# Retention output formed transposed with its states from one scan, and the search's exact step and key marking taken block by block behind the third pair's norm

## The chip, the cores and the metric

The kernel runs on one NeuronCore of a Trainium2 chip. The metric is the device time of one execution in microseconds (us). TensorE (PE) multiplies matrices, PEld is its weight load; VectorE (DVE), ScalarE (ACT) and GpSimd (POOL) work elementwise; SyncE (SP) issues DMAs. Each engine takes its instructions in a fixed order, and each waits for semaphores that others raise.

## The reference

One step of a decoder layer on 1024 new prompt tokens and 8 x 4 sample tokens, all in float32. From a normalised, modulated input h, one wide projection gives thirteen parts. Two branches use them and are merged by gates:

```python
# sparse attention: index scores choose 256 keys per query
scores = einsum(relu(qi @ ki.T), wi)          # [1024, 1024], causal
idx    = top_k(scores, 256)                   # keys of each query
y_a    = softmax(q @ k[idx].T / 8) @ v[idx] * silu(za)
# retention, 8 heads of 64, chunks of 128 tokens
scores = (q_c @ k_c.T) * decay_mask
out    = scores @ v_c + (q_c @ state) * q_decay
state  = exp(128 * lg) * state + (k_c * k_decay).T @ v_c
y_r    = group_norm(out) * g_ret * silu(zr)
x      = x + gate * ((sigmoid(ga) * (y_a @ w_pa) + sigmoid(gr) * (y_r @ w_pr)) @ w_out)
```

Outputs are the two token sets, their new keys, values and index keys, and the retention states.

## The kernel before

All of the wide projection runs on TensorE as products of split numbers (each float32 operand is a high and a low part): `project` streams 72 products of 128 x 352 per block of 128 columns (8 row blocks, 3 terms, 3 token chunks) into two banks `pj` in turn, and a `use` function takes each chunk out. `prefetch` loads the next block's weights (`ws`, an SP DMA) and splits them (`wh` on ScalarE, `wl` on VectorE or, one time in three, GpSimd, L195 and L196). After the index scores `SC` (prompt, blocks of 128 queries) and `SCS` (sample) stand in SBUF, three things run side by side: four gate blocks; the retention in four pairs of heads; and the search.

The search (`pick_all`) finds for each query the 256th largest score bit by bit, in 31 rounds. In each, VectorE counts for five blocks how many scores reach a candidate (`count`, L728), ScalarE does the same by signs for the last prompt block and the sample (`count_signs`, L735), and a few small VectorE instructions (L742, L744, L804, L806) make the next candidate. Then come `exact` (L755 to L770), which finds the exact score for the two blocks counted by signs, and `finish` (L775 to L784), which counts the scores above the threshold for all seven blocks and marks by block the keys that are out: equal to the threshold (L780), a running count of these (a scan, L781), two combining steps (L782, L783) and the mask `bi` or `bis` (L784). The sample's mask goes to memory (L823, L825) and is used after the retention, the prompt's masks in the attention later.

The retention takes the pairs p = 0 to 3. For each, `pair` projects keys, queries and values; GpSimd rotates keys and queries (L454 to L456); `to_tokens` turns keys and values by TensorE transposes (L426), which ScalarE copies out (`vtok`, `kd`: L465, L468); the gate part z follows (L477 to L479). Then:

- L485: 16 products, for 8 chunks and 2 heads, k decayed by v, into one bank `pk`, chunk after chunk.
- L487, L489: the states. Seven VectorE steps, each S[c] = S[c-1] * decay + pk[c].
- L496, L501: scores of each chunk, times a decay mask, into two tiles `sT`.
- L508, L511: the output `po`, with tokens on the partitions: 14 products q by state (weights are a 64 x 128 piece of q, 64 columns stream), then 16 products of scores and values (weights are 128 x 128 scores, 64 columns stream).
- L513: one ScalarE copy puts `po` in `O`. The sample tokens' part follows (L517 to L540).
- L545 to L568: the group norm of `O`: mean, square, an inverse root in small VectorE steps, transposes back (L564), and L567, which multiplies by z's gate. L567's third instruction is the last of the pair on VectorE.

Behind each pair come a projection of attention queries (`split_rows`, L392, L393) and two gate blocks. Per pair a constant table `DM` of 128 x 320 numbers is loaded (L433); `RC` holds other constants, the decay of the states among them.

The order of each engine is written out by a planner (`schedule_with_timeline_sim=True`) that follows the program's order and its own timeline; the search is traced last (`back`, `drain`) and so fills what the retention leaves on VectorE and ScalarE. `together` and `tc.issue_after(x)` add edges: what is traced inside is put behind x on x's engine, without a semaphore.

Of the kernel before, what the change touches and what calls it, by code (L numbers as in the profile page):

```python
# [49 lines left out]
R_G, R_GS, R_MB, R_ALL = 0, 4, 8, 16  # L50

M_D, M_S, M_ALL = 0, 256, 320


def shape_constants():
# [32 lines left out]
    for h in range(8):  # L88
# [3 lines left out]
        m[q, :32, M_S + 32 * i:M_S + 32 * i + 32] = np.where(ok, np.exp(lg[h] * f(-4.0)), 0)  # L92
        for a, decay in enumerate((np.exp(lg[h] * (size - f(1.0) - step)) * f(0.125), np.exp(lg[h] * (step + f(1.0))))):
            rot[q, a, rows, :TT] = cos * decay[None, :]
            rot[q, a, rows, TT:] = sin * decay[None, :]
        r[rows, R_G + q] = np.exp(lg[h] * f(128.0))
# [23 lines left out]
def _hybrid_step(ctx, tc, A, outs, dbg):  # L120
# [22 lines left out]
    def pt():  # L143
        return ps.tile([128, 512], F32, name="pt", bufs=2)
# [257 lines left out]


    def retention(gp):
        with ExitStack() as s3:
# [4 lines left out]
            nc.gpsimd.memset(O[:, 8], 0.0)  # L410
            for p in range(4):
                pair(rp, RC, O, p)
# [16 lines left out]
    def pair(rp, RC, O, p):  # L429
# [53 lines left out]
        S = rp.tile([128, 8, 64], F32, name="S")  # L483
        pk = pt().rearrange("p (c e) -> p c e", e=64)
        together([lambda c=c, i=i: nc.tensor.matmul(pk[head[i], c], kd[:, c, head[i]], vtok[:, c, head[i]], start=True, stop=True)  # L485
                  for c in range(8) for i in (0, 1)])
        nc.vector.tensor_copy(S[:, 0], pk[:, 0])  # L487
        for c in range(1, 8):
            nc.vector.scalar_tensor_tensor(S[:, c], S[:, c - 1], RC[:, R_G + p:R_G + p + 1], pk[:, c], op0=OP.mult, op1=OP.add)  # L489
        nc.sync.dma_start(st_out[0, 0, 2 * p:2 * p + 2].rearrange("h d e -> (h d) e"), S[:, 7])  # L490


        sT = []
        for g in (0, 1):
# [12 lines left out]
        po = pl().rearrange("p (i c e) -> p i c e", i=2, c=8)  # L507
        together([lambda c=c, i=i: nc.tensor.matmul(po[:, i, c], qT[head[i], 128 * c:128 * c + 128], S[head[i], c - 1], start=(c == 7), stop=False)  # L508
                  for c in range(7, 0, -1) for i in (0, 1)])
        for g in (0, 1):  # L510
            together([lambda c=c, i=i: nc.tensor.matmul(po[:, i, c], sT[g][:, i, c % 4], vtok[:, c, head[i]], start=False, stop=(c == 7))  # L511
                      for c in range(4 * g, 4 * g + 4) for i in (0, 1)])
        nc.scalar.copy(O[:, :8].rearrange("p c i e -> p i c e"), po)  # L513
# [45 lines left out]
        for g in range(3):  # L559
# [7 lines left out]
            nc.vector.scalar_tensor_tensor(yT[:, sl], p_[:, :n], gT[:, p:p + 1], zsT[:, sl], op0=OP.mult, op1=OP.mult)  # L567
# [736 lines left out]
```

## Time and profile before

| | us |
|---|---|
| median of 3 runs (lowest to highest) | 1173.57 (1172.87 to 1173.94) |
| profiled execution | 1169.95 |
| its span, first to last instruction | 1168.1 |
| busy PE, DVE, ACT, POOL | 1104.2, 669.1, 452.8, 329.6 |
| mean granted TensorE clock | 0.98 |

The slices of the page, 29.2 us each, show where things lie: TensorE is at nine tenths or more in nearly all, and in slice 15 (409 to 438 us) at five tenths; VectorE is at nine tenths from about 175 to 440 us, with the search, and at one to three tenths for a while behind it.

```profile
## 2 busy tenths in 40 slices
PE   4999999999989959999998999999999999989997
...
DVE  6865349999999998113332222211237767477755
ACT  5465445555555311222243333212326666343211
POOL 2413006023311700160332222053114433376000
PEclk9999999999999987999999999999999999999999
```

### The profile page before, as it was taken

To read this page: it belongs to the slowest core of one execution; us is meant where nothing else is said; L and a number is where in the kernel's file an instruction comes from. 1 tells how busy PE (TensorE), PEld (TensorE's weight loads), DVE (VectorE), ACT (ScalarE), POOL (GpSimd) and SP (SyncE) were. 2 spreads that over 40 slices of the span, in tenths; PEclk is the share of its full clock that TensorE was granted. 3 is DMA by queue.
4 is the path that set the end of the run, shared out by engine and by line. 5 is a ranking of instruction groups with operands and counts; after the bars stand their busy time and mean duration, and the time that the engine had idled before them with its cause. 6 is when DMAs were issued, how large, how long until landed. Compare 5 with 4: busy or idle time off the path is not lost. (4 is left out here: it accounts for less than half of the span.)

```text
span 1168.1 us, 20306 instructions
## 1 busy us (share of the span) xinstructions
PE 1104.2 (95%) x8040; PEld 1008.5 (86%) x8040; DVE 669.1 (57%) x1599; ACT 452.8 (39%) x874; POOL 329.6 (28%) x258
## 2 busy tenths in 40 slices
PE   4999999999989959999998999999999999989997
PEld 3899989999879959999998999877888888888786
DVE  6865349999999998113332222211237767477755
ACT  5465445555555311222243333212326666343211
POOL 2413006023311700160332222053114433376000
PEclk9999999999999987999999999999999999999999
DMA  9913234145222422341687567589889841395221
GB/s 306 255 33 109 74 105 139 38 126 140 84 79 93 148 58 80 101 120 29 220 269 237 178 205 213 154 294 305 266 245 237 233 135 55 123 299 176 106 97 54
DMA packets 157892, 181.51 MB, mean 155 GB/s; under 512 B 18837, under 2 KB 129501, under 8 KB 156710
## 3 DMA queue, kind: packets, MB, share of 16 engines
q1 hardware_dynamic: 147864, 144.51, 41.7%
q0 software_dynamic: 9856, 35.66, 9.2%
q8 instruction: 63, 1.03, 0.4%
q14 instruction: 31, 0.25, 0.1%
q10 hardware_dynamic: 78, 0.06, 0.0%
HBM read 137.81 MB, written 38.60 MB: 151 GB/s over the span
## 5 line engine op out<-in xcount | busy, mean ns | idle before, releaser
L209 PE MATMUL pj<-hh,wh 128*128 128x352 f32 x1176 | 387.7, 330 | 7.6 <-ACT kx L395 3.0
L211 PE MATMUL pj<-hh,wl 128*128 128x352 f32 x1176 | 383.1, 326 | 0.0
L210 PE MATMUL pj<-hl,wh 128*128 128x352 f32 x1176 | 382.6, 325 | 0.0
L209 PEld LDWEIGHTS pj<-hh,wh 128*128 128x128 f32 x1176 | 223.0, 190 | 17.1 <-issue 6.0
L210 PEld LDWEIGHTS pj<-hl,wh 128*128 128x128 f32 x1176 | 223.7, 190 | 3.3 <-issue 2.5
L211 PEld LDWEIGHTS pj<-hh,wl 128*128 128x128 f32 x1176 | 223.0, 190 | 3.9 <-issue 3.4
L728 DVE TENSOR_SCALAR_CACHE_REDUCE eq<-sc,cand 128x896 bf16<-128x896 f32 (+4 forms) x155 | 135.7, 875 | 2.3
L196 POOL TENSOR_TENSOR wl<-ws,wh 128x1024 fp32r<-128x1024 f32 (+1 forms) x33 | 63.6, 1930 | 190.9 <-ACT wh L195 172.6
L195 ACT CAST wh<-ws 128x1024 fp32r<-128x1024 f32 (+1 forms) x65 | 61.1, 940 | 108.4 <-PE pj L210 66.9
L196 DVE TENSOR_TENSOR wl<-ws,wh 128x1024 fp32r<-128x1024 f32 x32 | 39.9, 1247 | 86.8 <-ACT wh L195 86.8
L1065 POOL TENSOR_SCALAR lg<-lg,st 128x1024 f32<-128x1024 f32 (+7 forms) x64 | 47.5, 749 | 75.3 <-DVE st L1064 69.6
L735 ACT ACTIVATE ra<-sc,cand 128x1024 bf16<-128x1024 f32 x31 | 35.6, 1149 | 64.9 <-DVE cand L806 64.9
L911 POOL DMA_INDIRECT kv<-in_cache_k,idx x32 | 30.9, 966 | 102.0 <-PE str L941 84.0
L1063 ACT ACTIVATE lg<-lg,st 128x1024 f32<-128x1024 f32 (+7 forms) x64 | 49.5, 775 | 21.4 <-DVE st L1062 21.2
L943 DVE COPY kt<-str 128x512 f32<-128x512 f32 x32 | 22.1, 689 | 61.3 <-PE str L941 57.6
L911 POOL DMA_INDIRECT kv<-in_cache_v,idx x32 | 31.4, 981 | 71.0 <-PE sx L969 41.8
L1241 PE MATMUL pj<-wol,MH 128*128 128x512 f32 (+1 forms) x136 | 51.2, 377 | 0.0
L1240 PE MATMUL pj<-woh,MH 128*128 128x512 f32 (+1 forms) x136 | 51.2, 377 | 0.0
L1242 PE MATMUL pj<-woh,ML 128*128 128x512 f32 (+1 forms) x136 | 51.2, 377 | 0.0
L574 ACT ACTIVATE raw<-pj 128x352 f32<-128x352 f32 x48 | 22.1, 460 | 71.9 <-PE pj L211 68.7
L1078 PE MATMUL tr<-C,lg 128*128 128x128 f32 x288 | 43.8, 276 | 1.3 <-ACT pT L1080 0.5
L1078 PEld LDWEIGHTS tr<-C,lg 128*128 128x128 f32 x288 | 33.7, 140 | 8.7 <-ACT pT L1080 1.9
(337 smaller groups left out, 2055.6 us busy)
## 6 DMA issues: line engine op xcount, KB each, us to landing
ws<-in_w_in SPq DMA_DIRECT2D x51, 512.0 KB
TG<-raw SPq DMA_DIRECT2D x16, 528.0 KB
rot<-in_rot SPq DMA_DIRECT2D x8, 1056.0 KB
wa<-in_w_ada SPq DMA_DIRECT2D x16, 512.0 KB
u<-TG SPq DMA_DIRECT2D x8, 528.0 KB
RT<-u SPq DMA_DIRECT2D x8, 528.0 KB
t<-TG SPq DMA_DIRECT2D x8, 528.0 KB
u<-RT SPq DMA_DIRECT2D x8, 528.0 KB
```

Of the source, the lines that this page charges most:

```text
L195: nc.scalar.copy(wh[:, :, :n], ws[:, :, :n])
L196: (nc.vector if len(order) % 3 else nc.gpsimd).tensor_sub(wl[:, :, :n], ws[:, :, :n], f32(wh[:, :, :n]))
L209: nc.tensor.matmul(p, wh[:, k], HH[k][:, sl], start=(k == 0), stop=False)
L210: nc.tensor.matmul(p, wh[:, k], HL[k][:, sl], start=False, stop=False)
L211: nc.tensor.matmul(p, wl[:, k], HH[k][:, sl], start=False, stop=(k == KT - 1))
L728: nc.vector.tensor_scalar(junk[:n, :W], sc, thr[:n, j:j + 1], 0.0, op0=op, op1=OP.add, accum_out=cnt[:n, j:j + 1])
L911: nc.gpsimd.indirect_dma_start(out=t.rearrange("p s c -> p (s c)"), out_offset=None, in_=cache.rearrange("g (r s) h d -> (g r) (s h d)", s ...
L1063: nc.scalar.activation(l, l, AF.Exp, bias=st[:, 2:3], scale=0.125, accum_out=st[:, 3:4])
L1078: nc.tensor.transpose(x[:, 128 * (j - j0):128 * (j - j0) + 128], lg[:, j % 2, 128 * (j // 2):128 * (j // 2) + 128], ident)
L1240: nc.tensor.matmul(x, MH[:, k, tk], wh[:, k], start=(k == 0), stop=False)
L1241: nc.tensor.matmul(x, MH[:, k, tk], wl[:, k], start=False, stop=False)
L1242: nc.tensor.matmul(x, ML[:, k, tk], wh[:, k], start=False, stop=(k == KT - 1))
```

## The change

*States from one scan.* L485's products write `pk` with the chunk as the innermost index (every eighth word of the bank). One VectorE scan over 512 columns, S[j] = m[j] * S[j-1] + pk[j], makes all states; the factors m, zero where a chunk row begins, are a new part of `DM` (now 832 columns), and the column of decays leaves `RC`. Two ScalarE copies per pair put the states into a tile `SD` that is cleared once for the retention and holds for each chunk a 128 x 128 block with the two heads on its diagonal. The last state goes out from `SD`, one DMA per head.

*Output transposed.* `po` now has the heads' channels on the partitions and tokens along the bank: 7 products of a whole `SD` block with q, then 16 of values (128 x 64 weights) with scores (128 columns stream). By halves, ScalarE copies `po` to SBUF, four transposes turn it, and ScalarE copies it into `O`.

*The search's end.* `exact` takes one block (its small steps on one column), `finish` too (its count and remainder for this block, then the same five steps). `pick_all` traces exact(1), exact(0) and finish(6) to finish(0) behind the third pair's last norm step (`normed[2]`, L567) on VectorE.

```diff
@@ -47,9 +47,9 @@
 C_HM = C_SB8 + 16
 C_ALL = C_HM + 32
-R_G, R_GS, R_MB, R_ALL = 0, 4, 8, 16
-M_D, M_S, M_ALL = 0, 256, 320
+R_GS, R_MB, R_ALL = 0, 4, 12
+M_D, M_S, M_G, M_ALL = 0, 256, 320, 832
 def shape_constants():
@@ -90,10 +90,11 @@
         rows = slice(64 * i, 64 * i + 64)
         m[q, :, M_D + 128 * i:M_D + 128 * i + 128] = np.where(df >= 0, np.exp(lg[h] * f(-128.0)), 0)
         m[q, :32, M_S + 32 * i:M_S + 32 * i + 32] = np.where(ok, np.exp(lg[h] * f(-4.0)), 0)
+        m[q, rows, M_G:M_G + 512] = np.where(np.arange(512)[None, :] % 8 > 0, np.exp(lg[h] * f(128.0)), 0)
         for a, decay in enumerate((np.exp(lg[h] * (size - f(1.0) - step)) * f(0.125), np.exp(lg[h] * (step + f(1.0))))):
             rot[q, a, rows, :TT] = cos * decay[None, :]
             rot[q, a, rows, TT:] = sin * decay[None, :]
-        r[rows, R_G + q] = np.exp(lg[h] * f(128.0))
         r[rows, R_GS + q] = np.exp(lg[h] * f(4.0))
     r[:32, R_MB:R_MB + 8] = (t[:, None] // 4 == b[None, :]).astype(f)
     return c, r, m, rot
@@ -400,6 +401,8 @@
             nc.sync.dma_start(d[128 * p:128 * p + 128], f32(t[:, :T]))
     TG = dram.tile([2 * D, TT], F32, name="TG")
+    normed = {}
     def retention(gp):
         with ExitStack() as s3:
@@ -408,8 +411,10 @@
             nc.sync.dma_start(RC, A["rcs"])
             O = rp.tile([128, 9, 2, 64], F32, name="O")
             nc.gpsimd.memset(O[:, 8], 0.0)
+            SD = rp.tile([128, 8, 128], F32, name="SD")
+            nc.gpsimd.memset(SD, 0.0)
             for p in range(4):
-                pair(rp, RC, O, p)
+                pair(rp, RC, O, SD, p)
                 split_rows(gp, O_QA + 128 * p, p, QD, qs)
                 gates(gp, (4 + 2 * p, 5 + 2 * p))
@@ -426,7 +431,7 @@
                 nc.tensor.transpose(p[:n, t - 4 * g], src[:, t * 128:t * 128 + n], ident)
             use(4 * g, m, 128 if g < 2 else NS, p)
-    def pair(rp, RC, O, p):
+    def pair(rp, RC, O, SD, p):
         flat = lambda t: t.rearrange("p t c -> p (t c)")[:, :TT]
         head = [slice(64 * i, 64 * i + 64) for i in (0, 1)]
         DM = rp.tile([128, M_ALL], F32, name="dm")
@@ -480,14 +485,15 @@
         project(O_ZR + 128 * p, use_z)
-        S = rp.tile([128, 8, 64], F32, name="S")
-        pk = pt().rearrange("p (c e) -> p c e", e=64)
-        together([lambda c=c, i=i: nc.tensor.matmul(pk[head[i], c], kd[:, c, head[i]], vtok[:, c, head[i]], start=True, stop=True)
+        S = rp.tile([128, 512], F32, name="S")
+        pk = pt()
+        by_chunk = pk.rearrange("p (e c) -> p c e", c=8)
+        together([lambda c=c, i=i: nc.tensor.matmul(by_chunk[head[i], c], kd[:, c, head[i]], vtok[:, c, head[i]], start=True, stop=True)
                   for c in range(8) for i in (0, 1)])
-        nc.vector.tensor_copy(S[:, 0], pk[:, 0])
-        for c in range(1, 8):
-            nc.vector.scalar_tensor_tensor(S[:, c], S[:, c - 1], RC[:, R_G + p:R_G + p + 1], pk[:, c], op0=OP.mult, op1=OP.add)
-        nc.sync.dma_start(st_out[0, 0, 2 * p:2 * p + 2].rearrange("h d e -> (h d) e"), S[:, 7])
+        nc.vector.tensor_tensor_scan(S, DM[:, M_G:M_G + 512], pk, 0.0, op0=OP.mult, op1=OP.add)
+        for i in (0, 1):
+            nc.scalar.copy(SD[head[i], :, head[i]], S[head[i]].rearrange("p (e c) -> p c e", c=8))
+            nc.sync.dma_start(st_out[0, 0, 2 * p + i], SD[head[i], 7, head[i]])
         sT = []
@@ -504,13 +510,22 @@
             sT.append(t)
-        po = pl().rearrange("p (i c e) -> p i c e", i=2, c=8)
-        together([lambda c=c, i=i: nc.tensor.matmul(po[:, i, c], qT[head[i], 128 * c:128 * c + 128], S[head[i], c - 1], start=(c == 7), stop=False)
-                  for c in range(7, 0, -1) for i in (0, 1)])
+        po = pl()
+        together([lambda c=c: nc.tensor.matmul(po[:, 128 * c:128 * c + 128], SD[:, c - 1], qT[:, 128 * c:128 * c + 128],
+                                               start=(c % 4 == 3), stop=False) for c in range(7, 0, -1)])
         for g in (0, 1):
-            together([lambda c=c, i=i: nc.tensor.matmul(po[:, i, c], sT[g][:, i, c % 4], vtok[:, c, head[i]], start=False, stop=(c == 7))
+            together([lambda c=c, i=i: nc.tensor.matmul(po[head[i], 128 * c:128 * c + 128], vtok[:, c, head[i]], sT[g][:, i, c % 4],
+                                                        start=False, stop=(c % 4 == 3))
                       for c in range(4 * g, 4 * g + 4) for i in (0, 1)])
-        nc.scalar.copy(O[:, :8].rearrange("p c i e -> p i c e"), po)
+        oT = flat(big(rp, "tmp"))[:, :1024]
+        for g in (0, 1):
+            half = slice(512 * g, 512 * g + 512)
+            nc.scalar.copy(oT[:, half], po[:, half])
+            x = pt()
+            for j in range(4):
+                c0 = 512 * g + 128 * j
+                nc.tensor.transpose(x[:, 128 * j:128 * j + 128], oT[:, c0:c0 + 128], ident)
+            nc.scalar.copy(O[:, 4 * g:4 * g + 4].rearrange("p t i e -> p (t i e)"), x)
         qm = rp.tile([128, NB, NS], F32, name="qm")
@@ -564,7 +579,7 @@
                 nc.tensor.transpose(p_[:, (t % 4) * 128:(t % 4) * 128 + n], y2[:n, t], ident[:n, :n])
             n = 512 if g < 2 else NS
             sl = slice(512 * g, 512 * g + n)
-            nc.vector.scalar_tensor_tensor(yT[:, sl], p_[:, :n], gT[:, p:p + 1], zsT[:, sl], op0=OP.mult, op1=OP.mult)
+            normed[p] = nc.vector.scalar_tensor_tensor(yT[:, sl], p_[:, :n], gT[:, p:p + 1], zsT[:, sl], op0=OP.mult, op1=OP.mult)
         nc.sync.dma_start(YR[128 * p:128 * p + 128], yT)
@@ -747,41 +762,41 @@
                 for j, (sc, bi, n, W) in enumerate(AB):
                     nc.vector.tensor_scalar(dst[:n, NV + j:NV + j + 1], cnt[:n, NV + j:NV + j + 1], W - 510.5, no, op0=OP.is_gt, op1=OP.mult)
-        def exact():
+        def exact(j):
+            sc, bi, n, W = AB[j]
+            c = slice(NV + j, NV + j + 1)
+            t, lw, fl = base.bitcast(F32)[:, c], low[:, c], flag[:, c]
+            nc.vector.tensor_scalar(lw, t, 0.0, None, op0=OP.is_lt)
+            nc.vector.scalar_tensor_tensor(lw, t, 1.1754943508222875e-38, lw, op0=OP.is_ge, op1=OP.add)
+            nc.vector.tensor_tensor(t, t, lw, op=OP.mult)
+            count(base.bitcast(F32), OP.is_gt, [(NV + j, AB[j])])
+            up = tp.tile([128, LK], F32, name="eq", bufs=1)
+            ra = tp.tile([128, LK], F32, name="ra", bufs=1)
+            nc.vector.tensor_scalar(up[:n, :W], sc, t[:n], 3.4e38, op0=OP.is_le, op1=OP.mult)
+            nc.vector.tensor_tensor_reduce(out=ra[:n, :W], in0=up[:n, :W], in1=sc, scale=1.0, scalar=3.4e38,
+                                           op0=OP.add, op1=OP.min, accum_out=lw[:n])
+            nc.vector.tensor_scalar(fl, cnt[:, c], 255.5, None, op0=OP.is_ge)
+            nc.vector.tensor_tensor(lw, lw, fl, op=OP.mult)
+            nc.vector.tensor_scalar(fl, fl, -1.0, 3.4e38, op0=OP.add, op1=OP.mult)
+            nc.vector.tensor_tensor(lw, lw, fl, op=OP.add)
+            nc.vector.tensor_tensor(t, t, lw, op=OP.max)
+        def finish(j):
+            sc, bi, n, W = (VB + AB)[j]
             thr = base.bitcast(F32)
...
+            count(thr, OP.is_gt, [(j, (sc, bi, n, W))])
+            nc.vector.tensor_scalar(rem[:, j:j + 1], cnt[:, j:j + 1], -1.0, float(TOPK), op0=OP.mult, op1=OP.add)
+            eq = tp.tile([128, LK], F32, name="eq", bufs=1)
+            ra = tp.tile([128, LK], F32, name="ra", bufs=1)
+            t = thr[:n, j:j + 1]
+            nc.vector.tensor_scalar(eq[:n, :W], sc, t, None, op0=OP.is_equal)
+            nc.vector.tensor_tensor_scan(ra[:n, :W], eq[:n, :W], eq[:n, :W], 0.0, op0=OP.add, op1=OP.bypass)
+            nc.vector.scalar_tensor_tensor(ra[:n, :W], ra[:n, :W], rem[:n, j:j + 1], eq[:n, :W], op0=OP.is_gt, op1=OP.mult)
+            nc.vector.scalar_tensor_tensor(ra[:n, :W], sc, t, ra[:n, :W], op0=OP.is_lt, op1=OP.add)
+            nc.vector.tensor_scalar(bi, ra[:n, :W], MASKNEG, None, op0=OP.mult)
         nc.vector.memset(BI[1], 0.0)
         for b in (0, 1):
@@ -804,8 +819,12 @@
                 nc.vector.tensor_tensor(base, base, inc, op=OP.bitwise_xor)
                 if k > 0:
                     nc.vector.tensor_scalar(cand, base, 1 << (k - 1), None, op0=OP.bitwise_xor)
-            exact()
-            finish()
+            with tc.issue_after(normed[2].ins):
+                exact(1)
+                exact(0)
+                for j in range(NP - 1, -1, -1):
+                    finish(j)
         back.append(pick_all)
         gates(gp, range(4))
```

## Rows read from the trace of the kernel before

**Rows 1.** Busy time of each engine over the whole span (the page, part 1).
```profile
PE 1104.2 (95%) x8040; PEld 1008.5 (86%) x8040; DVE 669.1 (57%) x1599; ACT 452.8 (39%) x874; POOL 329.6 (28%) x258
```

**Rows 2.** Who TensorE waited for, 90 to 700 us: total, times, longest.
```profile
PE pl L508 <- DVE S L489: 12.6, 1, 12.6
PE pt L426 <- ACT tmp L441: 4.1, 2, 2.4
...
PE pj L209 <- ACT raw L574: 1.0, 1, 1.0
```

**Rows 3.** Table by stage: stretch, length, busy time of each engine, clock, DMA.
```profile
388.50:455.50 67.00, 54.38 (x398) 52.10 (x396) 66.19 (x89) 11.39 (x22) 16.95 (x8) 0.82 0.26 77
478.50:529.60 51.10, 51.10 (x327) 50.64 (x325) 4.80 (x4) 12.68 (x24) 22.40 (x11) 1.00 0.37 105
```

**Rows 4.** VectorE in order of time, third pair and search's end: start, us, instruction.
```profile
388.55 2.33 DVE L755 TENSOR_SCALAR low<-base 128x2 f32<-128x2 f32 x1
...
415.54 4.39 DVE L781 TENSOR_TENSOR_SCAN ra<-eq 32x1056 f32<-32x1056 f32 x1
...
430.32 0.22 DVE L487 COPY S<-pt 128x64 f32<-128x64 f32 x1
...
436.49 1.21 DVE L781 TENSOR_TENSOR_SCAN ra<-eq 128x512 f32<-128x512 f32 x1
...
438.46 0.27 DVE L489 SCALAR_TENSOR_TENSOR S<-S,rc,pt 128x64 f32<-128x64 f32 x1
...
454.88 0.61 DVE L784 TENSOR_SCALAR bi<-ra 128x896 bf16<-128x896 f32 x1
```

**Rows 5.** TensorE in order of time, third pair's products and those after them.
```profile
414.50 1.15 PE L485 MATMUL pt<-vtok,kd 128*64 128x64 f32 x32
...
438.88 3.25 PE L508 MATMUL pl<-S,qrT 64*128 64x64 f32 x28 [12.62 <-DVE S L489]
442.06 7.09 PE L511 MATMUL pl<-vtok,tmp 128*128 128x64 f32 x32
...
450.07 0.49 PE L209 MATMUL pj<-hh,wh 128*128 128x352 f32 x1
450.37 0.49 PE L210 MATMUL pj<-hl,wh 128*128 128x352 f32 x1
```

**Rows 6.** TensorE in order of time, fourth pair.
```profile
524.53 1.03 PE L426 MATMUL pt<-C,krT 128*128 128x128 f32 x8
...
529.58 1.15 PE L485 MATMUL pt<-vtok,kd 128*64 128x64 f32 x32
...
538.04 1.78 PE L508 MATMUL pl<-S,qrT 64*128 64x64 f32 x28
539.75 3.79 PE L511 MATMUL pl<-vtok,tmp 128*128 128x64 f32 x32
```

**Rows 7.** Chain that ended last, in order of time: one of the attention's products.
```profile
900.14 2.12 PE po L1095 x36
```

**Rows 8.** ScalarE in order of time, first pair.
```profile
207.23 0.59 ACT L468 COPY kd<-pt 128x512 f32<-128x512 f32 x1
...
218.94 1.15 ACT L735 ACTIVATE ra<-sc,cand 128x1024 bf16<-128x1024 f32 x1 [4.92 <-DVE cand L806]
```

**Rows 9.** Groups by line on VectorE, 388 to 456 us: busy, mean ns, idle before.
```profile
L196 DVE TENSOR_TENSOR wl<-ws,wh 128x1024 fp32r<-128x1024 f32 x2 | 2.4, 1214 | 0.0
...
L527 DVE TENSOR_TENSOR ss<-pl,dm 32x64 f32<-32x64 f32 x1 | 0.2, 205 | 0.0
```

**Rows 10.** GpSimd in order of time, beside the old and the new place.
```profile
415.04 2.68 POOL L196 TENSOR_TENSOR wl<-ws,wh 128x1024 fp32r<-128x1024 f32 x1 [6.42 <-ACT wh L195]
...
498.74 2.45 POOL L454 TENSOR_TENSOR krT<-krT,rot 128x1056 f32<-128x1056 f32 x1 [14.15 <-DMA tmp<-krT]
```

**Rows 11.** VectorE in order of time, last norm step of third and fourth pair.
```profile
478.12 0.25 DVE L567 SCALAR_TENSOR_TENSOR tmp<-pt,gT,zsT 128x32 f32<-128x32 f32 x1 [2.74 <-PE pt L564]
...
570.40 0.25 DVE L567 SCALAR_TENSOR_TENSOR tmp<-pt,gT,zsT 128x32 f32<-128x32 f32 x1 [2.71 <-PE pt L564]
```

More of the change, by code (lines that the diff above doesn't have):

```diff
@@ L748, in reached @@
                     nc.vector.tensor_scalar(dst[:n, NV + j:NV + j + 1], cnt[:n, NV + j:NV + j + 1], W - 510.5, no, op0=OP.is_gt, op1=OP.mult)
-        def exact():
-            thr = base.bitcast(F32)
-            nc.vector.tensor_scalar(low[:, aa], thr[:, aa], 0.0, None, op0=OP.is_lt)
-            nc.vector.scalar_tensor_tensor(low[:, aa], thr[:, aa], 1.1754943508222875e-38, low[:, aa], op0=OP.is_ge, op1=OP.add)
-            nc.vector.tensor_tensor(thr[:, aa], thr[:, aa], low[:, aa], op=OP.mult)
-            count(thr, OP.is_gt, [(NV + j, x) for j, x in enumerate(AB)])
-            for j, (sc, bi, n, W) in enumerate(AB):
-                up = tp.tile([128, LK], F32, name="eq", bufs=1)
-                ra = tp.tile([128, LK], F32, name="ra", bufs=1)
-                c = slice(NV + j, NV + j + 1)
-                nc.vector.tensor_scalar(up[:n, :W], sc, thr[:n, c], 3.4e38, op0=OP.is_le, op1=OP.mult)
-                nc.vector.tensor_tensor_reduce(out=ra[:n, :W], in0=up[:n, :W], in1=sc, scale=1.0, scalar=3.4e38,
-                                               op0=OP.add, op1=OP.min, accum_out=low[:n, c])
-            nc.vector.tensor_scalar(flag[:, aa], cnt[:, aa], 255.5, None, op0=OP.is_ge)
-            nc.vector.tensor_tensor(low[:, aa], low[:, aa], flag[:, aa], op=OP.mult)
-            nc.vector.tensor_scalar(flag[:, aa], flag[:, aa], -1.0, 3.4e38, op0=OP.add, op1=OP.mult)
-            nc.vector.tensor_tensor(low[:, aa], low[:, aa], flag[:, aa], op=OP.add)
-            nc.vector.tensor_tensor(thr[:, aa], thr[:, aa], low[:, aa], op=OP.max)
@@ L772, in finish @@
-        def finish():
-            thr = base.bitcast(F32)
-            count(thr, OP.is_gt, enumerate(VB + AB))
-            nc.vector.tensor_scalar(rem, cnt, -1.0, float(TOPK), op0=OP.mult, op1=OP.add)
-            for j, (sc, bi, n, W) in reversed(list(enumerate(VB + AB))):
-                eq = tp.tile([128, LK], F32, name="eq", bufs=1)
-                ra = tp.tile([128, LK], F32, name="ra", bufs=1)
-                t = thr[:n, j:j + 1]
-                nc.vector.tensor_scalar(eq[:n, :W], sc, t, None, op0=OP.is_equal)
-                nc.vector.tensor_tensor_scan(ra[:n, :W], eq[:n, :W], eq[:n, :W], 0.0, op0=OP.add, op1=OP.bypass)
-                nc.vector.scalar_tensor_tensor(ra[:n, :W], ra[:n, :W], rem[:n, j:j + 1], eq[:n, :W], op0=OP.is_gt, op1=OP.mult)
-                nc.vector.scalar_tensor_tensor(ra[:n, :W], sc, t, ra[:n, :W], op0=OP.is_lt, op1=OP.add)
-                nc.vector.tensor_scalar(bi, ra[:n, :W], MASKNEG, None, op0=OP.mult)
+        def exact(j):
[16 more added lines that the diff above has]
+            nc.vector.tensor_tensor(t, t, lw, op=OP.max)
```

## The prediction

> **What bounds the kernel.** Read the busy shares first: TensorE is busy for 95% of the span and no other engine passes 57% [rows 1]. So an edit counts by TensorE work that it takes away, or by a gap in it that it closes. Then read who TensorE waited for in the stretch that the change touches: one wait is far above the rest, 12.6 us of the third pair's product with the state (L508) for VectorE's state steps (L489); the others before it are five groups from 4.1 down to 1.0 us, 10.6 in all [rows 2]. The table by stage says why. From 388.5 to 455.5 VectorE is busy for 66.19 of 67 us and the clock is 0.82; in the stretch from the third pair's last norm step to the fourth pair's state product it is busy for 4.80 of 51.10 [rows 3]. VectorE's instructions show the cause: L755, the first of the exact step, starts at 388.55; the third pair's first state step (L487) at 430.32, although its product (L485) had ended at 415.65; the sixth step, which L508 needs, at 438.46 [rows 4, 5]. Search work sits between any two of them. L508 starts at 438.88 after 12.62 us of nothing.
>
> That gap costs more than itself, because TensorE comes back slow: L508 takes 3.25 us, in the undisturbed fourth pair 1.78; L511 7.09 against 3.79; the projection products after them follow each other at 0.30 (450.07, 450.37), 12 in all, where the fourth pair's stage has 327 instructions in 51.10 us, 0.16 each [rows 3, 5, 6]. Over these: 1.47 + 3.30, and 12 x 0.14, 1.6. [...]
>
> **The change, part by part.** The sum is made against the profiled execution, 1169.95 us (span 1168.1 and 1.85 around it). The median of the runs shown is 1173.57, 3.6 higher; I carry the difference over to it.
>
> *Third pair's gap.* The exact step and the marking of keys go behind the third pair's norm on VectorE, so nothing of the search stands before that pair's state any more, and VectorE, which ends its counting at about 388, has 25 us of spare time ahead of it. The 12.6 and the 6.4 us go: **-19.0**. Next to be late there is the new chain, short since VectorE and ScalarE are both free.
>
> *TensorE's own work, for each pair.* L511's 16 products (32 instructions) load 64 columns and stream 128 where they loaded 128 and streamed 64. The attention's L1095 has this form: 36 instructions in 2.12 us, 0.059 each [rows 7], so 1.9 instead of 3.79. L508's 28 instructions become 14 with full 128x128 weights; at L511's rate for such weights (3.79/32 = 0.118) that is 1.7 against 1.78. Added are eight transposes; eight in one go take 1.03 [rows 6], in two goes with two run-outs I take 1.3. Sum -0.7, four pairs **-2.8**. The state product L485 now writes every eighth word of its bank. No row shows a strided write by TensorE; below, nothing excludes a gain but nothing suggests one, so 0; above, as much again as it takes now, 1.15 [rows 6], or 4.6 for four pairs. I take 0 because L485's 32 instructions are issued at 0.036 each, and keep 4.6.
>
> [...]
>
> *State chain.* VectorE loses one copy (0.22) and seven steps of some 0.27 (2.1) and gains one scan over 512 columns, 1.21 by the scan of that width in the marking [rows 4]. ScalarE gains two copies into the block-diagonal tile and, for the output, four half-copies instead of one over 1024 columns; at 0.59 for 128x512 that is some 2.5 more per pair [rows 8]. In the first two pairs both engines are also in the search, and ScalarE stands up to 4.92 us on the next candidate (L735) with later copies queued behind it; the products with the state, the transposes and the projections behind them on TensorE wait for those copies. Against that the chain of six steps, spread over 8 us by search work, becomes one. Bounds for both pairs together: -3 (part of the 10.6 us of small waits goes) and +4 (one extra stand of nearly that length). I take **+1.0**.
>
> *The moved block.* Its length: from 388.55 to the end of L784 at 455.49 is 66.9 us [rows 4]. Of that, seven groups of other work, L196's 2.4 the largest and L527's 0.2 the smallest, make 9.6 [rows 9]. Six of its instructions are 11.5 us longer than their like; the first is L755 (2.33 for two columns, where 0.16 is usual), the last the scan at 415.54 (4.39, 2.27 for the same width less 32) [rows 4], and each overlaps a GpSimd instruction, as that scan overlaps L196 at 415.04 [rows 10]. Left are 45.8; per-block small steps, 14 more at 0.22, make it 48.8. It moves past no queue but VectorE's and issues no DMA; SyncE's copy of the first mask (L823, L825) is later with it but read only after the retention, and the weight loads queued behind it are one projection (72 products at 0.16) ahead: 0.
>
> Where it now starts: the fourth pair's norm ends 41.1 us after its state product starts (570.65 - 529.58) [rows 6, 11]; the third's will too, less 4 us for the shorter chain (8.5 us from L485 to L508 become 4.5). The fourth pair's state product comes 115.1 us after the third's (414.50 to 529.58), less 19.0 and 0.7: 95.4. So the block has 95.4 - 37.1 = 58.3 us, 1.1 more until the state product has ended, and about 3 more while TensorE does the scores. It needs 48.8 and the 4.8 of other work; but GpSimd's 22.40 us of rotation and weight work now lie beside it [rows 3, 10]. Beside the old place GpSimd was busy for 16.95 us and cost VectorE 11.5, a share of 0.68; so 15.2 more. 68.8 against 62.4: the fourth pair's scan comes 6.4 us late, and TensorE waits there. With the slow clock after it in the old proportion (6.4 x 6.4/12.6 = 3.3): **+9.7**. Bounds: 0, when GpSimd's work meets the counts, which it does not lengthen, or lies outside; and, with all 22.4 lost, 13.6 of gap and 6.4 of clock, 20.0.
>
> *The rest.* The larger per-pair table (832 columns for 320) is loaded while the pair before is still being finished, the clearing of the tile comes once on an idle GpSimd, the state goes out in eight DMAs for four: 0, and about 1 us if that cover fails. Behind the retention TensorE stays the bound, so I let the gain through.
>
> Sum: -19.0 - 2.8 + 1.0 + 9.7 = **-11.1**, 1158.9 for the profiled execution, **1162.5** by the median.
>
> **The rivals.**
> *A: the block fits.* GpSimd's instructions fall beside the counts, or the norm ends earlier than 37 us. For it: VectorE has only 4.8 us of other work there [rows 3]. Against it: 22.40 us of GpSimd. No new gap: 1162.5 - 9.7 = 1152.8.
> *B: the wait moves and grows; slower.* Place: the fourth pair's L508. The norm ends as late as the third pair's did in the profile, 39.5 us after L508 against 32.6 [rows 5, 6, 11], so 6.9 later, and all of GpSimd's work is lost: a gap of 13.6 + 6.9 = 20.5 and 6.4 of clock, 26.9; -19.0 - 2.8 + 1.0 + 26.9 = +6.1, 1179.7. It decides from a gap of about 14.4 us on. Against it: VectorE has nothing beside that norm any more.
> *C: the strided state product costs.* 4.6 more than the forecast, 1167.1. [...]
> *D: the first two pairs wait for ScalarE.* Each pair has three new hand-overs (tile, output, transposed output), each stands 2 us on the search's candidates: 12 instead of 1, 1173.5. For it: L735's stand of 4.92 [rows 8]. Against it: TensorE has projections to put between.
> That the block would not move at all is excluded by the order edge to the norm.
>
> **How the numbers follow.** A measurement here can tell about 0.2%, 2.3 us, from no change. Chances: forecast 0.42, A 0.27, B 0.09, C 0.10, D 0.12. Faster: nearly all of the forecast and of A, C less 0.02, 0.05 of D: 0.80. Same: the edges of all but A: 0.11. Slower: most of B and a rest of D: 0.09. The range runs from a little under A, where the first pairs also gain, 1151, to the upper end of D, 1174; B lies outside. The forecast's own range is 1157 to 1168.
>
> **What would show it.** Right: no wait at the third pair's L508, and clock 1.0 in its stage; L511 near 1.9 us; VectorE full from the third norm on, and a gap of 3 to 10 us before the fourth pair's L508 with VectorE's scan or ScalarE's copies as what ended it. Wrong: no gap there (A) or one over 14 us (B); L485 much over 1.15 us (C); new waits for ScalarE in the first two pairs that sum to over 5 us (D).

## The result and the profile after

The changed kernel takes 1155.31 us (median of 4 runs, 1153.97 to 1158.47), the kernel before 1173.22 beside it (4 runs, 1172.63 to 1173.94): a ratio of 0.9851, 95% interval [0.9828, 0.9874], 17.9 us less. Forecast were 1162.5 us with a range from 1151 to 1174. The profiled execution took 1154.27 us, against 1169.95 before and 1158.9 forecast for it. All lines below L430 have moved by a few; the state product L485 is L491, the product with the state L508 is L514, the scores' product L511 is L517.

The busy shares hardly move [rows 1]: TensorE is still the bound, busy for 14 us less. First the page's part 1, then who TensorE waited for from 90 to 700 us (total, times, longest).

```profile
PE 1090.3 (95%) x8016; PEld 993.7 (86%) x8016; DVE 674.0 (58%) x1585; ACT 465.1 (40%) x894; POOL 335.0 (29%) x259
```

```profile
PE pl L514 <- ACT SD L495: 12.6, 2, 11.4
PE pj L210 <- ACT qrT L446: 3.2, 2, 1.9
PE pt L431 <- ACT tmp L446: 2.5, 1, 2.5
PE pj L210 <- ACT qs L398: 1.6, 2, 0.9
PE pj L210 <- ACT kx L396: 1.2, 1, 1.2
PE pt L551 <- ACT O L528: 0.7, 1, 0.7
```

The 12.6 us stand there again as in [rows 2], by chance the same figure, but they are another wait: 11.4 of them belong to the fourth pair, and it is ScalarE's copies of the state that end it. TensorE in order of time shows both pairs: the third runs through, the fourth has the gap.

```profile
408.82 1.15 PE L491 MATMUL pt<-vtok,kd 128*64 128x64 f32 x32
...
414.53 1.72 PE L514 MATMUL pl<-qrT,SD 128*128 128x128 f32 x14
416.19 1.97 PE L517 MATMUL pl<-tmp,vtok 128*64 128x128 f32 x32
...
422.04 1.09 PE L527 MATMUL pt<-C,tmp 128*128 128x128 f32 x8
...
503.68 1.15 PE L491 MATMUL pt<-vtok,kd 128*64 128x64 f32 x32
...
520.91 3.35 PE L514 MATMUL pl<-qrT,SD 128*128 128x128 f32 x14 [11.35 <-ACT SD L495]
524.20 2.82 PE L517 MATMUL pl<-tmp,vtok 128*64 128x128 f32 x32
```

The table by stage (stretch, length, busy time of each engine, clock, DMA) shows why, beside [rows 3]: from the third pair's last norm step to the fourth pair's state product VectorE went from 4.80 us of work to 55.64 of 56.2, and in the next 23 us TensorE is busy for half.

```profile
447.50:503.70 56.20, 56.20 (x360) 55.74 (x358) 55.64 (x74) 13.61 (x26) 24.98 (x10) 1.00 0.37 107
503.70:527.00 23.30, 11.95 (x127) 11.07 (x128) 17.38 (x23) 3.65 (x6) 3.46 (x2) 0.71 0.16 44
```

VectorE in order of time gives the moved block: from 447.45 to 515.58, 68.1 us (68.8 forecast). The fourth pair's scan (L493) comes at 517.35, though its product had ended at 504.83. In the middle four lines show what makes the block long: three steps of the marking over 384 columns take 2.65, 2.72 and 1.95 us (0.62, 0.62 and 0.36 in the version without the rotation, below), a count over 512 takes its usual time (0.73; 0.74 in that version).

```profile
447.45 0.21 DVE L772 TENSOR_SCALAR low<-base 128x1 f32<-128x1 f32 x2
...
475.53 2.65 DVE L797 SCALAR_TENSOR_TENSOR ra<-ra,rem,eq 128x384 f32<-128x384 f32 x1
478.22 2.72 DVE L798 SCALAR_TENSOR_TENSOR ra<-sc,base,ra 128x384 f32<-128x384 f32 x1
480.86 0.73 DVE L743 TENSOR_SCALAR_CACHE_REDUCE eq<-sc,base 128x512 bf16<-128x512 f32 x1
...
481.53 1.95 DVE L799 TENSOR_SCALAR bi<-ra 128x384 bf16<-128x384 f32 x1
...
514.95 0.63 DVE L799 TENSOR_SCALAR bi<-ra 128x896 bf16<-128x896 f32 x1
...
517.35 1.22 DVE L493 TENSOR_TENSOR_SCAN S<-dm,pt 128x512 f32<-128x512 f32 x1
```

GpSimd in order of time has the rotation of the fourth pair's keys just there, and ScalarE the two copies that let TensorE go on.

```profile
474.60 3.16 POOL L459 TENSOR_TENSOR krT<-krT,rot 128x1056 f32<-128x1056 f32 x1 [15.77 <-DMA tmp<-krT]
477.73 2.80 POOL L460 TENSOR_TENSOR tmp<-tmp,rot 128x1056 f32<-128x1056 f32 x1
480.60 2.65 POOL L461 TENSOR_TENSOR krT<-krT,tmp 128x1056 f32<-128x1056 f32 x1
```

```profile
518.60 2.26 ACT L495 COPY SD<-S 64x512 f32<-64x512 f32 x2 [3.85 <-DVE S L493]
```

Both L797 and L798 end within half a microsecond of a GpSimd instruction's end (0.42 us behind L459's and 0.41 behind L460's). These two steps with two inputs took 2.65 and 2.72 us for 0.62, while the count (one tensor) beside L461 took 0.73 as elsewhere. But one tensor is no protection by itself: L799, the mask, has one and took 1.95 us for 0.36, until 0.23 us behind L461's end. What makes the one longer and not the other no run shows.

Where the time went is seen best by taking the same projection product in both traces and noting how much later it starts than in the kernel before (us, so earlier is negative; each time counts from its own trace's first instruction). The two parts of the change done alone, and the version with the old seven steps, are experiments below:

```
up to (before's time)               after    retention alone  search alone  seven steps
first pair's state, 200 us          -1.0         +0.4            -1.0          -0.1
first pair, 275 us                  -2.4         -1.0            +0.9          -2.0
second pair, 381 us                 -9.4         -8.2            +1.2          -3.8
third pair, 485 us                 -25.8         -6.3           -18.2         -23.6
fourth pair, 581 us                -12.7         -7.1            +0.5         -10.4
key copies, 726 us                 -15.9        -10.4            +0.6         -13.5
whole span                         -15.6         -9.9            +0.5          -9.7
```

What a stage gives is the difference of two rows: the first two pairs give the changed kernel 8.4 us (-9.4 less -1.0). Up to 200 us the kernels do the same, so the differences of up to 1.0 us there are the single execution's. The search's end alone leaves every engine's order up to 388 us as it was before, and still it loses 2.2 us in the first two pairs: differences of that size between two executions stand for nothing. The 8.4 us do stand: in the ten profiled versions here that have the whole of the new retention they lie between 8.0 and 8.7, and against the search's end alone they would be 2.2 more.

### The profile page after: what moved, and what is told of

Its sections match the earlier page's. It is cut to its first block, busy times and chain, and to the rows that moved or that the text cites. A ratio compares the mean times of both kernels' runs of the same rounds, so it can differ in the third digit from the quotient of the medians.

```text
span 1152.5 us, 20285 instructions
## 1 busy us (share of the span) xinstructions
PE 1090.3 (95%) x8016; PEld 993.7 (86%) x8016; DVE 674.0 (58%) x1585; ACT 465.1 (40%) x894; POOL 335.0 (29%) x259
## 5 line engine op out<-in xcount | busy, mean ns | idle before, releaser
L197 POOL TENSOR_TENSOR wl<-ws,wh 128x1024 fp32r<-128x1024 f32 (+1 forms) x33 | 63.1, 1913 | 174.8 <-ACT wh L196 156.4
L197 DVE TENSOR_TENSOR wl<-ws,wh 128x1024 fp32r<-128x1024 f32 x32 | 41.4, 1294 | 62.2 <-ACT wh L196 61.3
L962 ACT COPY kt<-str 128x512 f32<-128x512 f32 x32 | 18.8, 589 | 55.1 <-PE str L960 44.1
```

The source lines that it names most:

```text
L197: (nc.vector if len(order) % 3 else nc.gpsimd).tensor_sub(wl[:, :, :n], ws[:, :, :n], f32(wh[:, :, :n]))
```

## The experiments

The theory: both gaps are one thing, VectorE late for a pair's state because search work stands before it. The fourth pair's gap is the length of the moved block, stretched by GpSimd. Rival 1: the new chain of scan and ScalarE copies makes that gap. Rival 2: the change is worth what its order is worth, and the retention's new form adds little.

**The retention alone.** The old form of the exact step and of the marking stands in its old place.

```diff
-            with tc.issue_after(normed[2].ins):
-                exact(1)
-                exact(0)
-                for j in range(NP - 1, -1, -1):
-                    finish(j)
+            exact()
+            finish()
```

> One part alone: the new retention (strided state product, one scan, block-diagonal copies, transposed output), with the exact step and the marking left where the kernel before has them, in front of the third pair. Theory (VectorE's order sets both gaps): the third pair's product with the state (L514) waits again, for the scan that stands behind the search end: 14 to 18 us of gap and some 6 of slow clock after it, since only one step instead of six is late but the chain reaches TensorE earlier; no gap over 2 us at the fourth pair. Gain against before only from TensorE's work (3 us) and from the first two pairs and the third's shorter chain (6 to 10): 1161 us, 1157 to 1166. Rival 1 (the new chain of scan and ScalarE copies makes the gap of the fourth pair): that gap stays above 8 us here too. Rival 2 (the gain is the order's alone): 1171 to 1175.

1157.48 us, ratio 0.9875 [0.9852, 0.9899]. The gap is back at the third pair, 9.96 us, and the fourth pair has none (L514 at 528.91, 1.72 us). First TensorE, then VectorE, in order of time.

```profile
426.18 3.36 PE L514 MATMUL pl<-qrT,SD 128*128 128x128 f32 x14 [9.96 <-ACT SD L495]
```

```profile
421.96 0.73 DVE L795 TENSOR_SCALAR eq<-sc,base 128x1024 f32<-128x1024 f32 x1
422.62 1.20 DVE L493 TENSOR_TENSOR_SCAN S<-dm,pt 128x512 f32<-128x512 f32 x1
```

The place is as the theory has it, the size is not: 9.96 for 14 to 18. Rival 1 falls, and so does rival 2: most of the gain is here, without the move. What the move adds in the new retention, 0.9875 to 0.9851, can't be told from nothing: the intervals overlap.

**The search's end alone.** The old retention (state by seven steps, output not transposed); exact step and marking as changed.

```diff
-        nc.vector.tensor_tensor_scan(S, DM[:, M_G:M_G + 512], pk, 0.0, op0=OP.mult, op1=OP.add)
+        nc.vector.tensor_copy(S[:, 0], pk[:, 0])
+        for c in range(1, 8):
+            nc.vector.scalar_tensor_tensor(S[:, c], S[:, c - 1], RC[:, R_G + p:R_G + p + 1], pk[:, c], op0=OP.mult, op1=OP.add)
...
```

> The other part alone: the old retention (seven steps, output not transposed) with the exact step and the marking by block behind the third pair's norm. Theory: the third pair's gap of 12.6 us and its slow clock go (-19), and the fourth pair's product waits as in the changed kernel or a little longer, 12 to 16 us, since its seven steps follow the block; with its slow clock some 16 to 20. Nothing gained in the first two pairs: 1170 us, 1165 to 1175. Added to the retention alone, the two differences make about the whole (-18) or less. Rival 1 (the new chain makes the fourth pair's gap): no gap over 3 us here, time 1152 to 1157.

1170.17 us, ratio 0.9987 [0.9970, 1.0004]: no difference that can be told. The table says why: the third pair gave 19.4 us (19.0 forecast), the fourth took 18.7 back. Two waits stand there, TensorE in order of time:

```profile
523.07 0.66 PE L209 MATMUL pj<-hh,wh 128*128 128x352 f32 x1 [3.61 <-ACT zsT L480]
...
531.50 3.25 PE L510 MATMUL pl<-S,qrT 64*128 64x64 f32 x28 [7.47 <-DVE S L491]
534.68 7.09 PE L513 MATMUL pl<-vtok,tmp 128*128 128x64 f32 x32
```

So the move by itself only moved the gap. The theory holds; rival 1 expected no gap here.

**The changed kernel without the fourth pair's rotation** (for its queries and its keys; that pair's output is another).

```diff
-            nc.gpsimd.tensor_tensor(x, x, RT_[:, :TT], op=OP.mult)
-            nc.gpsimd.tensor_tensor(y, y, RT_[:, TT:], op=OP.mult)
-            nc.gpsimd.tensor_tensor(x, x, y, op=OP.add)
+            if p < 3: nc.gpsimd.tensor_tensor(x, x, RT_[:, :TT], op=OP.mult)
+            if p < 3: nc.gpsimd.tensor_tensor(y, y, RT_[:, TT:], op=OP.mult)
+            if p < 3: nc.gpsimd.tensor_tensor(x, x, y, op=OP.add)
```

> The changed kernel without the fourth pair's rotation of its queries and keys (three GpSimd instructions for each of the two are left out, so that pair's output is another). Theory (the moved block is long because VectorE loses time beside GpSimd): the block takes 55 to 60 us instead of 68.1, its steps in the stretches at 474 to 483 and 489 to 499 take their usual times, the fourth pair's gap of 11.35 us falls to 0 to 3, time 1143 to 1147. Rival 1 (the gap is the new chain's): gap stays over 8 us, time 1153 to 1156. Rival 2 (the block is too long by its own work): block over 63 us, gap about 7, time 1149 to 1152.

1141.46 us, ratio 0.9749 [0.9729, 0.9770]. VectorE in order of time: the block runs from 446.69 to 503.69, 57.0 us instead of 68.1, and L797 over 384 columns takes 0.62. TensorE has no gap.

```profile
446.69 0.21 DVE L772 TENSOR_SCALAR low<-base 128x1 f32<-128x1 f32 x2
...
474.77 0.62 DVE L797 SCALAR_TENSOR_TENSOR ra<-ra,rem,eq 128x384 f32<-128x384 f32 x1
...
503.07 0.62 DVE L799 TENSOR_SCALAR bi<-ra 128x896 bf16<-128x896 f32 x1
```

Six instructions of GpSimd, 18.3 us together, had cost VectorE 11.1 us net, a share of 0.61 (0.68 in the forecast). This is the theory shown: the same chain, no gap.

**The exact step not bound to the norm.** TensorE's, ScalarE's and GpSimd's order is that of the changed kernel.

```diff
+            exact(1)
+            exact(0)
             with tc.issue_after(normed[2].ins):
-                exact(1)
-                exact(0)
```

> The changed kernel, but the exact step of the two blocks that need it is not bound to the third pair's norm; only the marking is. TensorE's, ScalarE's and GpSimd's order is that of the changed kernel. Theory (VectorE is late for the fourth pair by the length of the bound block): the block is shorter by the exact step's 9 us, so the fourth pair's gap falls from 11.35 us to 1 to 4 and its slow clock with it; VectorE has idle time for the exact step ahead of the third pair, which is not late by it: 1143 to 1148. Rival 1 (the gap is the new chain's): no change of the gap, 1154 to 1157. Rival 2 (the exact step in front of the third pair delays that pair instead): a new gap of 4 to 9 us at the third pair's L514, 1150 to 1156.

1145.14 us, ratio 0.9779 [0.9759, 0.9799], as the theory had it; both rivals fall (third pair's L514 at 414.32 without a wait). The fourth pair's gap is gone altogether, but a new wait stands in its stage, for the lower half of a weight block that VectorE forms between two marking steps, all three beside GpSimd's rotation of the queries. TensorE, then VectorE, in order of time:

```profile
494.11 0.43 PE L212 MATMUL pj<-hh,wl 128*128 128x352 f32 x1 [3.64 <-DVE wl L197]
```

```profile
487.67 3.03 DVE L797 SCALAR_TENSOR_TENSOR ra<-ra,rem,eq 128x768 f32<-128x768 f32 x1
490.62 3.43 DVE L197 TENSOR_TENSOR wl<-ws,wh 128x1024 fp32r<-128x1024 f32 x1
```

**The block behind the fourth pair's norm**, whole, and in a second version its marking alone, with the exact step not bound. The diff is that of the first.

```diff
-            with tc.issue_after(normed[2].ins):
+            with tc.issue_after(normed[3].ins):
```

> The changed kernel with the whole block (exact step and marking) behind the fourth pair's norm instead of the third's. Theory (both gaps are VectorE late for a pair's state): no gap at either pair's L514; the fourth pair's 11.35 us and its 2.5 us of slow clock go, 13.9; behind that norm VectorE has 35 us of work in 140, so the block of some 57 to 60 us is hidden there. 1139 to 1144 if nothing else waits. Rival: SyncE stands on its copy of the first mask (L842) until that block is marked, about 10 us after the norm, with the weight loads of the gates queued behind it, and TensorE waits for the weights: 3 to 8 us of new waits, 1144 to 1150.

> Exact step not bound (as in the version with that alone, 1145.14) and the whole marking behind the fourth pair's norm. Theory: no gap at the third and fourth pair's L514, and the 3.6 us wait for the lower half of the weights (VectorE's L197 beside GpSimd's rotation) of that version goes too: 1138 to 1142. Rival: SyncE's stand on the first mask delays the gates' weights by 3 to 8 us: 1143 to 1149, no better than the exact step alone.

1178.38 us, ratio 1.0048 [1.0030, 1.0067], and 1177.19, 1.0029 [1.0012, 1.0046]: both slower than before, by 0.3 to 0.5%. A miss, by theory and rival alike. The gaps at the states are gone (no wait of TensorE from 400 to 560 us); it loses behind. The waits from 90 to 700 us, then VectorE and ScalarE in order of time, in the whole block's version:

```profile
PE pj L210 <- ACT kx L396: 13.6, 3, 9.4
```

```profile
574.03 0.52 DVE L394 TENSOR_TENSOR raw<-pj,raw 128x352 fp32r<-128x352 f32 x1
...
599.71 0.38 DVE L920 TENSOR_SCALAR idx<-gidx 128x8 int32<-128x8 int32 x4
```

```profile
574.58 0.45 ACT L396 COPY kx<-pj 128x352 f32<-128x352 f32 x1 [7.82 <-DVE raw L394]
```

In the changed kernel VectorE is busy for only 16.71 of the 60 us from 560 to 620, but each piece is awaited at once: ScalarE's copy of the new keys stands 7.82 us for VectorE's L394, queued behind marking. And the gathers' indices (L920) are made at 599.71 instead of 515.49, so that the gathers start at 600.14 instead of 555.10. From 800 to 900 us TensorE is then busy for 89.3 us, in the changed kernel for 96.8. In the whole block's version the projection products start 27.6 us earlier than before at 550 us, 16.1 at 650 and 14.9 at 780, and the whole span is 7.6 longer: more is lost behind 780 us than at the key copies. That this later loss comes from the late gathers was not tried by itself.

**Only the last two blocks behind the fourth norm.**

```diff
-                for j in range(NP - 1, -1, -1):
+                for j in range(NP - 1, 1, -1):
                     finish(j)
+            with tc.issue_after(normed[3].ins):
+                finish(1)
+                finish(0)
```

> The changed kernel with the marking of the last two blocks (1 and 0 in its order, 13 us) behind the fourth pair's norm, the rest behind the third's as it is. Theory: the block behind the third pair's norm ends at about 502 instead of 515.6, before the fourth pair's state product has ended (504.83), so the gap of 11.35 us and its slow clock go: 1139 to 1144, as with the rotation left out (1141.46). Rival (the fourth pair waits for something else besides): a gap over 4 us stays, 1146 to 1152.

1150.02 us, ratio 0.9799 [0.9781, 0.9816]. The fourth pair's gap is gone, as expected, but the time falls short of the 1139 to 1144 us: at 581 us the same projection product is 13.3 us earlier than in the changed kernel, at 726 still 7.4, over the whole span 2.7. Among the waits behind the fourth pair are 5.0 us for L396 (1.2 in the changed kernel) and 2.3 for the gathered keys, the loss of the version before in small.

**The old seven steps in the new retention.** The state product is contiguous again, and so is ScalarE's reading of the states.

```diff
-            nc.scalar.copy(SD[head[i], :, head[i]], S[head[i]].rearrange("p (e c) -> p c e", c=8))
+            nc.scalar.copy(SD[head[i], :, head[i]], S[head[i]])
...
```

> The changed kernel with the state formed as before it (contiguous state product, a copy and seven steps on VectorE), but the block-diagonal copies, the products with the state and the transposed output as changed. It tells which half of the retention's change gives the 7 us that the second pair loses beyond TensorE's own work. If it is the single scan (the seven steps are spread among the search's): the second pair's gain of about 6 us is gone and its products with the state wait 3 to 6 us; with a fourth pair's gap longer by 1 to 3 us, 1160 to 1166. If it is the output (two half-copies with transposes instead of one copy of 1024 columns): the second pair keeps it, 1155 to 1159.

1158.61 us, ratio 0.9877 [0.9858, 0.9896], 3.3 us more than the changed kernel with intervals that overlap. Between the two expectations: by the table the first two pairs keep 3.7 of their 8.4 us, so 4.7 go with the single scan, about twice what two executions of the same order can differ by there. In the second pair the seven steps end 12.3 us after their product (323.66 and 311.35), the scan 4.6 (313.92 and 309.27). But TensorE doesn't stand at that pair's product with the states, as the expectation had it. It stands 2.8 us for ScalarE's copies of the turned output (L530), and its clock from 325 to 345 us is 0.83, in the changed kernel 1.00. Tables by stage, this version and the changed kernel:

```profile
325.00:345.00 20.00, 17.23 (x144) 14.82 (x143) 19.12 (x48) 11.75 (x21) 4.48 (x2) 0.83 0.37 116
```

```profile
325.00:345.00 20.00, 19.11 (x144) 17.60 (x144) 19.15 (x63) 11.74 (x23) 4.52 (x2) 1.00 0.36 107
```

How the longer chain leads to that wait was not tried. The third pair gives most of the 4.7 back: the changed kernel, ahead of time, waits 1.9 us before it for ScalarE's L446 (the copy of the projected queries and keys), this version doesn't. What the rest of the second pair's gain comes from, the transposed output or the order that follows it, stays open, and so do the 3.8 us that this version loses behind 726 us.

**Where else the marking can stand.** In one version the last two blocks (the tail) go behind the fourth pair's second score mask (L507, `scored`); in the next the first block (the head) goes behind the halving of the inverse root in the third pair's norm (L570, `scaled`); in the last both are done. The exact step is not bound in any. The diff is that of the last, against the version with the exact step free.

```diff
+            with tc.issue_after(scaled[2].ins):
+                finish(NP - 1)
             with tc.issue_after(normed[2].ins):
-                for j in range(NP - 1, -1, -1):
+                for j in range(NP - 2, 1, -1):
                     finish(j)
+            with tc.issue_after(scored[3].ins):
+                finish(1)
+                finish(0)
```

> Exact step not bound, and the marking of the last two blocks behind the fourth pair's second score mask (L507), where VectorE has idle time between that pair's state and its norm; the other five stay behind the third pair's norm. Theory: the five end at about 487 us, in front of the fourth pair's lower weights, so that the 3.6 us wait for VectorE's L197 and its slow clock (5.4 together) that the exact step alone had left are gone; no gap at the fourth pair's state; the two late blocks take the idle time of the fourth pair's norm, which TensorE doesn't wait for: 1138 to 1142. Rival (the weights wait only moves, or the norm, later by up to 10 us, holds the gathers and the key copies as it did behind the fourth norm): 1145 to 1150.

> Exact step not bound, and the marking of the first block (7.5 us) behind the last small step of the third pair's norm (the halving of the inverse root, VectorE idle from 436.2 to 443.0); the other six behind the norm. Theory: the block behind the norm ends 7 us earlier, about 500, still beside GpSimd's rotation of the queries (486 to 496), where VectorE's L197 can stand behind a marking step again: the 5.4 us of the wait for the weights go in part or not at all, 1140 to 1146. Rival (an early block delays the norm's last step and with it everything bound to it): 1146 to 1150.

> Exact step not bound, first block marked early (behind the halving of the inverse root in the third pair's norm), the last two behind the fourth pair's score mask, four behind the third pair's norm. Theory: the four end at about 480; no wait at either pair's state nor for the weights: 1138 to 1142, the same as with the tail moved alone, since TensorE then has nothing left to wait for in these stages. Rival: as for the tail alone, 1145 to 1150.

The tail alone: 1145.75 us, ratio 0.9775 [0.9756, 0.9794], no better than the exact step alone and short of its expectation; the wait for the weights is gone, one of 2.0 us for ScalarE's L398 (the copy of the sample's attention queries) takes part of its place. The head alone: 1152.81, 0.9831 [0.9810, 0.9853], worse, against the expectation: with the head gone the weights' L197 stands behind four marking steps, and TensorE waits twice as long. Both: 1142.87, 0.9751 [0.9732, 0.9770], just above the 1138 to 1142 expected, below the changed kernel beyond the intervals, not told apart from the exact step alone. Waits from 90 to 700 us with the head alone, then VectorE in order of time with both:

```profile
PE pj L212 <- DVE wl L197: 7.1, 1, 7.1
```

```profile
477.56 1.95 DVE L197 TENSOR_TENSOR wl<-ws,wh 128x1024 fp32r<-128x1024 f32 x1 [7.36 <-ACT wh L196]
...
503.52 1.21 DVE L493 TENSOR_TENSOR_SCAN S<-dm,pt 128x512 f32<-128x512 f32 x1
```

With both, VectorE stands idle 7.36 us before it forms those weights, and the fourth pair's scan comes right after its product.

## Why the prediction was right, and where it was not

The direction, the two gaps and their engine were right; the sum came near because misses of both signs met, and that is luck. The third and fourth pairs together were to give 10.7 us and gave 3.3; most of the gain came from the first two pairs, which were to give 0.4. The median lies below the forecast's own range of 1157 to 1168 us and nearer to rival A's time (1152.8) than to the forecast's, but the trace has the forecast's gap and not A's missing one. In the profiled executions, term by term (forecast, measured from the table):

```
up to 200 us         0     -1.0     (the single execution's)
first two pairs    -0.4   -8.4     (-1.4 of TensorE's work and +1.0 of waits)
third pair        -19.7  -16.4     (-19.0 and -0.7)
fourth pair        +9.0  +13.1     (+9.7 and -0.7)
behind it           0     -2.9
sum               -11.1  -15.6
```

For the first two pairs, tables by stage, before and after:

```profile
183.00:240.00 57.00, 53.99 (x425) 51.00 (x424) 54.96 (x142) 31.82 (x57) 14.15 (x9) 0.97 0.31 92
...
300.00:350.00 50.00, 43.62 (x354) 40.21 (x353) 48.09 (x133) 28.59 (x54) 7.57 (x6) 0.97 0.29 84
```

```profile
183.00:240.00 57.00, 53.18 (x428) 50.02 (x427) 54.82 (x139) 34.49 (x64) 14.72 (x9) 1.00 0.35 101
...
300.00:350.00 50.00, 47.88 (x394) 44.90 (x394) 47.85 (x140) 31.48 (x57) 8.67 (x5) 1.00 0.32 95
```

- **First two pairs: the step that failed.** "+1.0" weighed ScalarE's new copies against a shorter chain and took the wrong side; the lower bound was -3, and measured are -8.4 with TensorE's own work in it, so about -7. The small waits fell from 10.6 us [rows 2] to 7.4 (2.5, 1.6, 0.7, the 1.4 of L446's that is not the third pair's and the 1.2 of L495's that is not the fourth's), and the clock, 0.97 before from 183 to 240 and from 300 to 350 us, is 1.00 in both, worth another 3.2 (0.03 of 107 us). That clock the forecast left out in these pairs. The forecast had one cause in it, a chain "spread over 8 us by search work" that "becomes one", but let the copies weigh more; in the version with the old steps that chain took 12.3 us, and 4.7 of the 8.4 us were gone. D (these pairs wait for ScalarE) did not come: its sign was new waits of over 5 us.
- **Third pair.** The gap is gone and nothing takes its place in that pair. The move alone is worth 19.4 us there, as forecast (19.0: 12.6 of wait, and 6.4 of slow clock that is the sum of 1.47, 3.30 and 1.6; the granted clock was 0.50 from 438.88 to 449.15 us and 0.53 from there to 453.20). In the changed kernel 3.3 are missing: TensorE, now ahead, waits 1.9 us for L446 and goes at 0.94 of the clock from 384 to 413 us. The clock need not follow that wait: the version with both has the same wait and 1.00 there.
- **TensorE's own work.** L514 and L517 take 3.63 us from start to end instead of 5.50, the transposes 1.09: -0.8 for a pair, -0.7 forecast. The state product takes 1.15 us as before, though it writes every eighth word of its bank: C falls, for this stride and 64 columns.
- **The moved block.** Its length was right, 68.1 for 68.8 us, and so was the share that GpSimd takes. The gap was 11.35 for 6.4: left out was the chain after the block, scan and copies (3.5 us from 517.35 to 520.86). The rest nearly cancels: 1.8 us of other VectorE work between block and scan, a window 2.1 us shorter than forecast, against 0.7 us less of block and 1.7 us more of work for TensorE to do meanwhile. The clock's share was 2.5 for 3.3. The gap lies above the 3 to 10 us that were to show the forecast right and below the 14 that were to show B. A (the block fits) needs what the versions with the exact step free show: 9 us less. B did not come here; the old retention with the same move went near it, 11.1 us of gap (7.47 and 3.61) and no gain.
- **Behind the retention.** "I let the gain through" was not quite so: the wait for the key copies falls from 3.0 to 1.2 us, with the new retention only. Why was not tried.

The medians differ by 17.9 and the profiled executions by 15.7; the 2.2 us between them lie within the runs' spread of 4.5.

## What to carry to other kernels

A block of work that is moved out of one wait has to be laid out at its new place with everything beside it: its own time (57.0 us without the rotation beside it), the engine that slows it (GpSimd's rotation, 11.1 us), and the chain that begins when it ends (3.5 us); here the move gained nothing in the old retention (0.9987) and nothing that can be told in the new one (0.9875 to 0.9851), and paid once the exact step was left out of the bound block (0.9779). An engine's idle share is no room by itself: behind the fourth norm VectorE had work for a quarter of the time (16.71 of 60 us), and each piece of it was awaited at once. Parts of a block that nobody waits for are best bound each to a place of its own; bound as one they stand in front of something.

## What the runs showed of the hardware

ScalarE's copy of 64x512 floats takes 1174 ns where it reads every eighth word and 618 where it reads in order (the groups of L495 and of the seven steps' L497; both write the same tile). The forecast had taken 590.

Behind the gap at the products with the state, TensorE's granted clock was back at 1.00 sooner in the new form. After 11.35 us of idle L514 and L517 took 2.5 us more than usual (granted clock 0.58 from 520.9 to 527.0 us), and the projections behind followed at 0.16 us at once, at clock 1.00 (527.0 to 531.0 us); after 9.96 us, with the retention alone, it was 1.9 us more. In the old form, after 12.62 us before the change and after 7.47 with the search's end alone, the products took 3.25 and 7.09 for 1.78 and 3.79 (clock 0.50 before the change), and the projections followed at 0.29 for some 4 us more (clock 0.53 before the change). The runs don't show which property of the products makes the difference.
